# Out projections and a pooling layer's input projection by seven products of quarters

## The chip, the cores and the metric

The kernel runs on one core of a Trainium2 chip. A core has a matrix engine (TensorE, PE in the profile; loading its stationary side is PEld), three engines that work on tiles in the on-chip memory SBUF (VectorE or DVE, ScalarE or ACT, GpSimd or POOL), and a queue engine (SyncE or SP) that here only starts transfers. Products go to a second memory, PSUM, which the matrix engine writes and VectorE and ScalarE read. The metric is the device time of one execution in microseconds.

## What is computed

Two layers over 1,024 tokens of 2,048 channels. Everything below concerns the two output projections and the second layer; the attention in front stays as it is but for what it leaves in DRAM.

```python
def _attention_layer(...):                      # layer 0
    ...
    y = jnp.concatenate([outA, outB], axis=-1) * jax.nn.silu(z)
    x = x + gate * _rmsnorm(y @ w_out, post_g)

def _pool_layer(...):                           # layer 1
    h = _rmsnorm(x, pre_g) * (1 + scale) + shift
    proj = h @ w_in                             # 2048 -> 4096: u and the gates
    y = _multiscale_pool(proj[..., :POOL_WIDTH], pool_w, pool_scale) * jax.nn.silu(proj[..., POOL_WIDTH:])
    x = x + gate * _rmsnorm(y @ w_out, post_g)

def _multiscale_pool(u, pool_w, pool_scale):    # windows 2, 4, 8, 16 for four groups of 512 channels
    ...                                         # centred mean over the window, less the token
    mixed = jnp.einsum('blgc,gcd->blgd', pooled, pool_w).reshape(B, L, POOL_WIDTH)
    return mixed * pool_scale
```

All numbers are float32.

## The kernel before

A product of two float32 matrices is made of three products of 12-bit parts: each side is split into a high part (a cast to fp32r on ScalarE, in `split`, L146) and a low part (the number less its high part, on VectorE or GpSimd, L149), and `PASSES` takes high by high, high by low and low by high.

Weights come from DRAM in `w_tiles`: up to 1,024 columns at a time into a raw tile `wr` (two buffers), split into `wh` and `wl` (eight buffers each). The layer before attention goes through `gemm` (L186) over blocks of 256 outputs.

Attention runs over 32 units (four groups of heads, eight blocks of 128 queries). Each unit turns weights (L850), multiplies them with the values (L904), multiplies the result by the gate over the softmax's sums (`gate_over_sums` on GpSimd, `gated` on VectorE), splits it into `yo` and stores both parts to DRAM (`yd`). The softmax's sums go by DRAM too: `ls` is stored to `lsd` and read back as `rs` on all partitions.

`out_proj` (products on L962) is called for each half of the tokens, 512 at a time: four column groups of 512, each over 16 chunks of 128 rows and four blocks of tokens, with the tokens stationary and 512 weight columns moving. Its end multiplies by the gate (L969), squares for the norm, and adds the residual (L1026 or L1149). After layer 0 the rows are normed (L1033), turned (L1062) and split again into `hT`; six blocks of layer 1's first gates (L1043) stand between, so that the second half's turning has products beside it. Layer 1 (`project1`, `pooled`) goes through `gemm` for both halves of the tokens at once, so each weight is read and split once. `pooled` adds by doubling (L1106) on VectorE and GpSimd in turn; the pool maps (`mx`) are products of `gemm` as well, and their result goes to DRAM as `y1d`.

A scheduler places the instructions on each engine; `keep_in_program_order` holds some of them in the order of the code. Loads stand in SyncE's queue (`load`), stores mostly in ScalarE's (`store`).

Of the kernel before, what the change touches and what calls it, by code (L numbers as in the profile page):

```python
# [17 lines left out]
P = 128  # L18
D = 2048
# [4 lines left out]
HL = L // NH  # L24
HD = 128
# [5 lines left out]
# A product of two float32 numbers, each cut exactly into two 12-bit parts.  # L31
# [4 lines left out]
LEAD = 28  # L36
# [9 lines left out]
BRIDGE = 6  # L46
PINS = (0,)
# Chunks of rows whose products ACT and Pool take, for shifts and scales.
# [3 lines left out]
def _constants():  # L52
# [7 lines left out]
    # Blocks of keys before, at and after the queries' own; the context's are all open.  # L60
# [18 lines left out]
def tile_backbone(ctx, tc, ins, out):  # L79
# [4 lines left out]
    # Sums of the modulation over the rows, still to be added up over the partitions.  # L84
# [19 lines left out]
    # Which of four lots of partitions a partition belongs to.  # L104
# [24 lines left out]
    # Scratch in DRAM.  # L129
# [8 lines left out]
    yd = [[dram([P, 4, 2, HL], f"yd{g}_{n}") for n in range(NH)] for g in range(4)]  # L138
    gpd = [[dram([1, 512], f"gpd{i}_{j}") for j in range(4)] for i in range(2)]
    x1d = [dram([P, D], f"x1d{t}") for t in range(8)]  # L140
    sd = [dram([P, HL], f"sd{m}") for m in range(BRIDGE)]
    y1d = [[dram([P, 4, 2, HL], f"y1d{g}_{n}") for n in range(NH)] for g in range(4)]

# [7 lines left out]
    wp = pool(ctx, "w")  # L151
# [39 lines left out]
    def newton(r, v, t):  # L191
        """r = 1 / sqrt(v), with a Newton step; t is room for it."""
# [7 lines left out]
    def rstd_rows(r, ss, tp, n, tag):  # L200
        """r = 1 / sqrt(ss / D + eps), elementwise."""
# [4 lines left out]
    def lots_of(d, a):  # L206
        """512 columns of d, as lots of 32 partitions with 128 columns of four of d's rows each."""
# [10 lines left out]
    # ---------------------------------------------------------------- attention weights  # L218
# [3 lines left out]
    # The pools of the units with an even number and, later, those with an odd one.  # L222
# [14 lines left out]
    def scores(u, kt, s_tile, c_tile, pinned=lambda i: i, pin=lambda i: i, band=None):  # L237
        """Attention weights of four heads' blocks of queries, with queries on the partitions."""
# [53 lines left out]
    # ---------------------------------------------------------------- layer 0: norms and projections  # L292
    with ExitStack() as st:
# [13 lines left out]
        # Small vectors, one column per 128 channels.  # L307
# [15 lines left out]
        # Scales and shifts of the attention layer's tokens, 512 channels at a time: products with the rows of the  # L323
        # weights, which the partitions add up first.
# [16 lines left out]
        def mod_add(accs, k, w, c, tp, shared):  # L341
            """Adds a chunk's products, on DVE or, the shared ones, on ACT and Pool."""
# [14 lines left out]
        def mod_columns(accs, n=4):  # L357
            """The sums over the partitions, a column per 128 channels."""
# [25 lines left out]
        # Tokens scaled by their root mean squares, then with channels on the partitions.  # L384
# [32 lines left out]
        def project(c0, nm, beside=None):  # L417
            """Products of blocks c0.. of w_in's columns with the tokens, by (block, half), with others between them."""
# [15 lines left out]
        def three(c0):  # L434
            """Three blocks, by halves, and the weights' tiles, two chunks of rows at a time."""
# [7 lines left out]
        # The first blocks of queries are made without the shifts, which come later and are added to the products.  # L443
# [79 lines left out]
        def rotated(src, n, g=None):  # L523
            """The rotary turn of a head's columns, times g."""
# [259 lines left out]
    def act_tile(k, n):  # L784
        """A chunk of 128 channels of one half of the tokens, in two parts."""
        return acts[n, k // 8].tile([P, 2, HL], F32R, tag="a", name="a")
# [392 lines left out]
```

## Time and profile before

| | |
|---|---|
| median of the runs (3) | 3113.52 us (3113.2 to 3115.45) |
| span of the profiled execution | 3115.6 us |
| PE busy | 2989.6 us (96%), 14,102 products |
| DVE busy | 1649.9 us (53%) |
| ACT busy | 1075.0 us (35%) |
| POOL busy | 424.1 us (14%), 327 instructions |
| DMA | 530.34 MB, mean 170 GB/s |

The page gives the busy time of each engine over one profiled execution. A matrix engine busy for 96% is a busy sequence of products, each of which overlaps the next; how long one takes in a sequence is read from the starts of its neighbours. Layer 0's projections and the modulation end near 1,140 us, attention near 1,605, the first out projection near 2,032, layer 1's projections near 2,756.

### The profile page before, as it was taken

How to read it: one execution, taken by the hardware profiler on the slowest of the kernel's cores; microseconds unless marked ns; L12 is line 12 of the kernel's file. 1: busy time of each engine (PE TensorE's matmuls, PEld its weight loads, DVE VectorE, ACT ScalarE, POOL GpSimd, SP SyncE). 2: the span in 40 equal slices, each digit the busy share in tenths (PEclk: the TensorE clock that was granted, in tenths of full speed). 3: DMA queues.
4: the chain of work that ended last, by engine and by line, in shares of the span. 5: the costliest groups of instructions: out<-in, count | busy, mean ns of one | idle time of the engine just before them, and what ended most of it. 6: DMA issues, size and time to landing. Idle time of an engine off the chain costs nothing.

```text
span 3115.6 us, 38559 instructions
## 1 busy us (share of the span) xinstructions
PE 2989.6 (96%) x14102; PEld 2481.0 (80%) x14102; DVE 1649.9 (53%) x2725; ACT 1075.0 (35%) x2073; POOL 424.1 (14%) x327
## 2 busy tenths in 40 slices
PE   5899999899999999999899999999999999999998
PEld 5677777787888788888778888888888888888887
DVE  7968877555235748888753363623332323322434
ACT  6542312221111147776642352522222221222332
POOL 4643413000001100001220040300000001000000
PEclk8989999999999999999999999999999999999999
DMA  8738776888467854445555544423222121355734
GB/s 289 242 126 252 215 247 219 254 289 260 171 235 253 267 177 124 136 125 159 153 170 164 214 138 157 156 65 111 85 91 75 48 101 49 129 176 172 250 104 163
DMA packets 373011, 530.34 MB, mean 170 GB/s; under 512 B 28644, under 2 KB 215894, under 8 KB 371670
## 3 DMA queue, kind: packets, MB, share of 16 engines
q1 hardware_dynamic: 287990, 445.81, 44.7%
q10 hardware_dynamic: 84832, 82.07, 7.7%
q8 instruction: 111, 1.82, 0.2%
q14 instruction: 78, 0.64, 0.1%
HBM read 428.88 MB, written 98.91 MB: 169 GB/s over the span
## 4 chain that ended last, share of the span: by engine, by line
PE 70%; DMA 13%; DVE 9%; issue 3%; ACT 2%; POOL 2%; SPq 0%; ACTq 0%; DVEq 0%; POOLq 0%
PE g L186 32%; PE g L962 21%; DMA mraw<-in_od_mod_w_dram 5%; DVE mac L355 5%; PE o L904 4%; DMA mraw<-in_ev_mod_w_dram 3%; PE mx L186 3%; PE s L254 3%; PE t L850 3%; PE g L1043 2%; DVE wl L149 1%; DMA lsd<-ls 1%; DMA wr<-in_od_w_out_dram 1%; DMA rs<-lsd 1%; PE c L260 1%
## 5 line engine op out<-in xcount | busy, mean ns | idle before, releaser
L149 DVE TENSOR_TENSOR wl<-wr,wh 128x512 fp32r<-128x512 f32 (+1 forms) x576 | 414.9, 726 | 852.6 <-ACT wh L146 835.4
L186 PE MATMUL g<-h,wh 128*128 128x512 f32 x2368 | 756.8, 400 | 8.1 <-ACT fe L477 5.8
L146 ACT CAST wh<-wr 128x512 fp32r<-128x512 f32 (+1 forms) x576 | 349.6, 615 | 1100.2 <-PE g L186 563.5
L962 PE MATMUL g<-wh,a 128*128 128x512 f32 x1920 | 594.4, 390 | 0.1
L186 PE MATMUL g<-a,wh 128*128 128x512 f32 x1856 | 571.0, 389 | 0.0
L186 PEld LDWEIGHTS g<-h,wh 128*128 128x128 f32 x2368 | 453.9, 194 | 100.7 <-POOL h L148 5.9
L186 PE MATMUL g<-h,wl 128*128 128x512 f32 x1184 | 473.9, 401 | 14.2 <-DVE wl L149 14.1
L355 DVE SCALAR_TENSOR_TENSOR mac<-mraw,csil,mac 128x512 f32<-128x512 f32 x423 | 364.5, 862 | 120.2 <-DMA mraw<-in_od_mod_w_dram 64.8
L962 PEld LDWEIGHTS g<-wh,a 128*128 128x128 f32 x1920 | 360.1, 188 | 75.5 <-ACT wh L146 0.8
L186 PEld LDWEIGHTS g<-a,wh 128*128 128x128 f32 x1856 | 348.3, 188 | 72.4
L962 PE MATMUL g<-wl,a 128*128 128x512 f32 x960 | 373.7, 389 | 0.0
L186 PE MATMUL g<-a,wl 128*128 128x512 f32 x928 | 360.7, 389 | 0.0
L186 PEld LDWEIGHTS g<-h,wl 128*128 128x128 f32 x1184 | 227.9, 193 | 67.0 <-DVE wl L149 19.9
L962 PEld LDWEIGHTS g<-wl,a 128*128 128x128 f32 x960 | 180.2, 188 | 37.2
L186 PEld LDWEIGHTS g<-a,wl 128*128 128x128 f32 x928 | 174.2, 188 | 36.3
L149 DVE TENSOR_TENSOR tl<-t,th 128x512 fp32r<-128x512 f32 x236 | 160.0, 684 | 39.5 <-ACT th L146 38.0
L146 ACT CAST th<-t 128x512 fp32r<-128x512 f32 x236 | 135.9, 584 | 110.6 <-PE t L850 109.3
L904 PE MATMUL o<-th,vt 128*128 128x512 f32 x472 | 156.3, 412 | 2.5 <-ACT th L146 2.5
L850 PE MATMUL t<-ident,p 128*128 128x128 f32 x944 | 139.0, 276 | 10.5 <-DVE tl L149 10.1
L850 PEld LDWEIGHTS t<-ident,p 128*128 128x128 f32 x944 | 114.8, 142 | 38.2 <-DVE tl L149 15.5
L537 POOL TENSOR_TENSOR ra<-ra,rt 128x512 f32<-128x512 f32 x40 | 64.7, 1619 | 553.1 <-DMA mraw<-in_ev_mod_w_dram 287.8
L1106 POOL TENSOR_TENSOR s<-s 128x541 f32<-128x541 f32 (+1 forms) x32 | 38.1, 1190 | 587.4 <-DVE s L1106 561.7
(221 smaller groups left out, 3357.2 us busy)
## 6 DMA issues: line engine op xcount, KB each, us to landing
mraw<-in_ev_mod_w_dram SPq DMA_DIRECT2D x192, 256.0 KB, 4.0
mraw<-in_od_mod_w_dram SPq DMA_DIRECT2D x192, 256.0 KB, 4.6
wr<-in_od_w_in_dram SPq DMA_DIRECT2D x76, 512.0 KB, 3.6
wr<-in_ev_w_in_dram SPq DMA_DIRECT2D x68, 512.0 KB, 4.6
mraw<-in_ev_mod_w_dram SPq DMA_DIRECT2D x64, 512.0 KB, 5.2
wr<-in_ev_w_out_dram SPq DMA_DIRECT2D x64, 512.0 KB, 3.8
wr<-in_od_w_out_dram SPq DMA_DIRECT2D x64, 512.0 KB, 4.8
qd<-hl ACTq DMA_DIRECT2D x64, 256.0 KB, 2.9
```

What stands on the lines that cost most here:

```text
L146: nc.scalar.copy(dst_h, src)
L149: (lo or nc.vector).tensor_tensor(dst_l, src, f32(dst_h), op=ALU.subtract)
L186: pin(nc.tensor.matmul(o, lhsT=w[a][:, kk, m * P : (m + 1) * P], rhs=rhs(n, k, b), start=(k == 0 and i == 0), stop=(k == kc - 1 and i == 2),))
L254: pin(nc.tensor.matmul(s[:, sl], lhsT=qt[:, h, a], rhs=kt[:, b, sl], start=i == 0, stop=i == 2))
L260: pinned(nc.tensor.matmul(cs[:, hh], lhsT=qt[:, h + hh, a], rhs=kt[:, b, L:], start=i == 0, stop=i == 2))
L355: nc.vector.scalar_tensor_tensor(accs[0], w, c, accs[0], op0=ALU.mult, op1=ALU.add)
L537: nc.gpsimd.tensor_tensor(a, a, t, op=ALU.add)
L850: pin(nc.tensor.transpose(t[:, h * P : (h + 1) * P], ps[h][:, i * P : (i + 1) * P], ident))
L904: pin(nc.tensor.matmul(outs[u], lhsT=vt[:, a, kb], rhs=b, start=(i == 0 and jj == 0), stop=(last and jj == 2)))
L962: nc.tensor.matmul(o, lhsT=y[k][:, a, t * P : (t + 1) * P], rhs=wt[b][:, k - k0, :], start=(k == 0 and i == 0), stop=(k == KC - 1 and i == 2),
L1043: mm = nc.tensor.matmul(o, lhsT=w[a][:, k - k0, m * P : (m + 1) * P], rhs=hT[k][0][:, b], start=(k == 0 and i == 0), stop=(k == KC - 1 and ...
L1106: eng.tensor_tensor(nx[:, lo + d :], cur[:, lo + d :], cur[:, lo : W - d], op=ALU.add)
```

## The change

Each of the out projections and layer 1's input projection is made of seven products of quarters in place of eight (the Strassen scheme in Winograd's form), over halves of the tokens. A block of 512 tokens, 512 outputs and all 2,048 rows is cut in two along each side. The left side then has eight slots, of which seven are used: four quarters of the tokens and four sums of them. The right side has seven: four quarters of the weights and sums of them. `seven` makes the products, 256 columns each, and adds them up out of seven PSUM banks.

The left sides go through DRAM (`ad`): attention, the turning of the normed tokens and the pool maps store their quarters and sums there (`left_sums`, on GpSimd), and `left_part` loads and splits them beside the last seven of the step before. `weights_of` makes the sums of the weights on GpSimd. Since one half of the tokens is done at a time, layer 1's weights are loaded and made twice. Gates and pooled tokens of layer 1 go through DRAM too (`gd`, `pod`), the pool maps stand between the projections' products (`map_steps`), and the rows' ends (`Beside`) beside the next out projection or the gates.

```diff
+    def left_sums(v):
+        for o, a, b, op in ((4, 6, 7, ALU.add), (2, 4, 0, ALU.subtract), (3, 0, 6, ALU.subtract), (5, 1, 2, ALU.subtract)):
+            nc.gpsimd.tensor_tensor(v[o], v[a], v[b], op=op)
...
         def gated(u, o, zt):
-            y = ap.tile([P, 4 * P], F32, tag="y", name="y", bufs=1)
-            nc.vector.tensor_tensor(y, o, zt.rearrange("p h q -> p (h q)"), op=ALU.mult)
-            yo = ap.tile([P, 2, 4 * P], F32R, tag="yo", name="yo", bufs=1)
-            split(yo[:, 0], yo[:, 1], y, "act", nc.gpsimd if u >= YP else None)
-            for t in range(2):
-                load(yd[g][n // 4][:, :, t, (n % 4) * P : (n % 4 + 1) * P], f32(yo[:, t]).rearrange("p (h q) -> p h q", q=P))
+            tp, ti = n % 2, n // 2 % 2
...
+            nc.vector.tensor_tensor(
+                sa[:, :, 6 * ti : 6 * ti + 2, :], o.rearrange("p (k i q) -> p k i q", k=2, i=2),
+                zt.rearrange("p (k i) q -> p k i q", k=2), op=ALU.mult,
+            )
+            if ti:
+                left_sums([sa[:, :, i, :] for i in range(8)])
+                for k in range(2):
+                    load(ad[0][n // 4][g // 2][:, 2 * (g % 2) + k, :, tp * P : (tp + 1) * P], sa[:, k])
...
+    def left_part(d, q):
+        left_tiles(q)
+        for s0 in range(0, 8, 2):
+            raw = staged()
+            slots = [s for s in (s0, s0 + 1) if s != 6]
+            for s in slots:
+                load(raw[:, 2 * (s - s0) : 2 * (s - s0) + 2], d[q // 2][:, 2 * (q % 2) : 2 * (q % 2) + 2, s, :])
+            for s in slots:
+                a = left[s][q]
+                v = raw[:, 2 * (s - s0) : 2 * (s - s0) + 2].rearrange("p k t -> p (k t)")
+                split(a[:, 0], a[:, 1], v, lo=nc.gpsimd if s % 2 else None)
+    def weights_of(w, kp, c0):
+        raw = wq.tile([P, 2, 2, QT], F32, tag="wr", name="wr", bufs=3)
...
+        t = wq.tile([P, 3, QT], F32, tag="wt", name="wt", bufs=2)
+        for o, a, b, op in (
+            (t[:, 1], raw[:, 1, 1], raw[:, 1, 0], ALU.subtract),
+            (t[:, 0], t[:, 1], raw[:, 0, 0], ALU.add),
+            (raw[:, 1, 0], raw[:, 1, 0], raw[:, 0, 0], ALU.subtract),
+            (t[:, 2], raw[:, 0, 1], t[:, 0], ALU.subtract),
+        ):
+            nc.gpsimd.tensor_tensor(o, a, b, op=op)
+        for i, v in ((0, raw[:, 0]), (2, t[:, 0:2]), (1, raw[:, 1]), (3, t[:, 2:3])):
+            made[i] = split_weights(v)
+    def seven(w, c0, tokens_still, q, done):
+        banks = [psg.tile([P, 2, QT], F32, tag="g", name="g") for _ in SEVEN]
+        for kp in range(8):
+            parts = weights_of(w, kp, c0)
+            for i, (slot, tile_, place) in enumerate(SEVEN):
+                a, o = left[slot][kp // 2], banks[i]
+                for v in range(2):
+                    for n_, (x, y) in enumerate(PASSES):
...
+                        tc.keep_in_program_order(nc.tensor.matmul(
+                            o[:, v], lhsT=lhsT, rhs=rhs, start=(kp == n_ == v == 0), stop=(kp == 7 and n_ == 2), skip_group_check=True,
+                        ))
+                if kp == 7:
...
+                        add(q(0, 0), o, q(1, 0), op=ALU.add)
...
+    def out_proj(ev, w, gps, ss, og):
...
+                for tp in range(2):
+                    square(ev, c[:, tp], ss[:, 2 * ti + tp, cp : cp + 1])
+                nc.gpsimd.tensor_tensor(c, c, gp.to_broadcast([P, 2, HL]), op=ALU.mult)
...
+    def attention_turn(ev, n, og):
+        for kp in range(8):
+            for tp in range(2):
+                sa = staged().rearrange("p a (b t) -> p (a b) t", b=2)
...
+                left_sums([sa[:, i] for i in range(8)])
+                to = ad[1][n][kp // 4][:, kp % 4, :, tp * P : (tp + 1) * P]
+                store(to[:, 0:6], sa[:, 0:6])
+                store(to[:, 7], sa[:, 7])
+                yield
...
+        for cp, kp in out_proj(ev, w_outs[0], gpd[0], ss, og):
+            if cp == 3 and kp % 2:
+                left_part(ad[1][0] if n else ad[0][1], kp // 2)
+            beside()
+        beside.set(attention_rows(ev, n, ss, og), attention_turn(ev, n, og))
```

The weights have two tags: double tiles `wh`, `wl` of 512 columns with four buffers and single ones of 256 with one (`WBUFS = 1, 4`); the staging tiles (`xr`) have two, `left` one per slot and quarter.

The order of the instructions at three places. TensorE at the end of attention, before (o are the attention's products; g the out projection's, with 512 weight columns moving):

```order
L904 MATMUL o<-th,vt 128x512 x2
L904 MATMUL o<-tl,vt 128x512
L962 MATMUL g<-wh,a 128x512
L962 MATMUL g<-wl,a 128x512
L962 MATMUL g<-wh,a 128x512 x2
```

And after (a_14553 to a_14555 are the first three slots of the left side):

```order
L913 MATMUL o<-th,vt 128x512 x2
L913 MATMUL o<-tl,vt 128x512
L1021 MATMUL g<-wh,a_14553 128x256
L1021 MATMUL g<-wl,a_14553 128x256
L1021 MATMUL g<-wh,a_14553 128x256 x2
L1021 MATMUL g<-wl,a_14553 128x256
L1021 MATMUL g<-wh,a_14553 128x256
L1021 MATMUL g<-wh,a_14554 128x256
```

The same place in the sequence now has six products of 256 columns per slot, two blocks of three passes.

GpSimd from the end of attention to the second half of the tokens, before (zt and yo are attention's; og the normed rows; a the turned tokens):

```order
L866 TENSOR_TENSOR zt<-zt,rs 128x512
L149 TENSOR_TENSOR yo<-y,yo 128x512
L1033 TENSOR_SCALAR og<-og,s_15887 128x512 x4
L1033 TENSOR_SCALAR og<-og,s_15929 128x512 x4
L1033 TENSOR_SCALAR og<-og,s_15971 128x512 x4
L1033 TENSOR_SCALAR og<-og,s_16013 128x512 x4
L148 TENSOR_SCALAR a<-nw 128x512 x16
```

And after, in the first out projection's last seven of the first half (wt and wr are the weights' sums, a_ the left side's low parts, og<-og,gp the gate):

```order
L1092 TENSOR_TENSOR og<-og,gp 128x1024
L998 TENSOR_TENSOR wr<-wr 128x256
L152 TENSOR_TENSOR a_16499<-xr,a_16499 128x512
L998 TENSOR_TENSOR wt<-wr,wt 128x256
L998 TENSOR_TENSOR wt<-wr 128x256
L152 TENSOR_TENSOR a_16501<-xr,a_16501 128x512
L998 TENSOR_TENSOR wt<-wt,wr 128x256
L998 TENSOR_TENSOR wr<-wr 128x256
L998 TENSOR_TENSOR wt<-wr 128x256
L152 TENSOR_TENSOR a_16502<-xr,a_16502 128x512
```

Where GpSimd had nothing between attention and the first norms, it now has the sums of every step's weights, with the left side's low parts among them.

SyncE's queue in the last units of attention, before (ls, rs: the softmax's sums; yd: the gated result; zt: a later unit's gate):

```order
L289 DMA lsd_153<-ls 128x4
L876 DMA yd_1_163<-yo 512x1x128
L918 DMA rs<-lsd_153 128x512
L876 DMA yd_1_163<-yo 512x1x128
L865 DMA zt<-zd_1_123 128x512
L289 DMA lsd_154<-ls 128x4
```

And after, from the same unit on, to the start of the out projection (ad: the left sides; xr: their staging tiles; gp: the gate; wr: the weights):

```order
L293 DMA lsd_153<-ls 128x4
L927 DMA rs<-lsd_153 128x512
L865 DMA zt<-zd_1_123 128x512
L293 DMA lsd_154<-ls 128x4
L927 DMA rs<-lsd_154 128x512
L293 DMA lsd_155<-ls 128x4
L927 DMA rs<-lsd_155 128x512
L1080 DMA gp<-gpd_0_156 128x512
L885 DMA ad_1_1_175<-sa 128x8x128 x4
L974 DMA xr<-ad_0_0_172 128x2x256 x5
L990 DMA wr<-in_ev_w_out_dram 128x2x256
```

The store that stood between a unit's lsd and rs now stands behind rs, and the first loads of the left side stand behind attention's last stores.

## Rows read from the trace of the kernel before

**Rows 1.** Busy time by stretch: start:end, length, each engine, granted clock, DMA share.
```profile
1400.00:1600.00 200.00, 183.72 (x1130) 159.36 (x1128) 149.60 (x372) 136.42 (x329) 43.48 (x31) 0.98 0.52 148
1607.00:3107.00 1500.00, 1498.64 (x6658) 1237.41 (x6656) 541.90 (x946) 428.79 (x799) 99.74 (x99) 1.00 0.39 131
3107.00:3116.00 9.00, 0.00 (x0) 0.00 (x0) 3.98 (x12) 0.89 (x3) 0.00 (x0) 0.72 0.33 127
```

**Rows 2.** The chain that ended last, pieces: start us, length us, what.
```profile
1542.15 4.66 DMA yd<-yo
1548.77 4.11 DMA lsd<-ls
...
1607.28 191.04 PE g L962 x842
...
2144.58 11.19 PE mx L186 x48
```

**Rows 3.** Timeline of TensorE near 905 us: start us, length, what.
```profile
902.05 0.63 PE L186 MATMUL g<-h,wh 128*128 128x512 f32 x2
...
907.51 0.40 PE L186 MATMUL g<-hc,wh 128*128 128x256 f32 x2
...
908.93 0.63 PE L186 MATMUL g<-h,wh 128*128 128x512 f32 x2
```

**Rows 4.** Instructions of single lines: duration ns least/median/most, first and last start.
```profile
L149 DVE TENSOR_TENSOR wl<-wr,wh x576: 545/691/1783, 44.8 to 3052.3; 128x512 fp32r<-128x512 f32 x181, 128x384 fp32r<-128x384 f32 x11
L149 DVE TENSOR_TENSOR tl<-t,th x236: 659/685/693, 1146.2 to 1605.4; 128x512 fp32r<-128x512 f32 x118
L149 POOL TENSOR_TENSOR hl<-ra,hl x40: 1268/1676/1842, 245.2 to 1079.1; 128x512 fp32r<-128x512 f32 x40
L149 POOL TENSOR_TENSOR hl<-zt,hl x4: 737/966/1191, 938.8 to 1080.7; 128x256 fp32r<-128x256 f32 x4
L537 POOL TENSOR_TENSOR ra<-ra,rt x40: 1260/1726/2321, 242.9 to 1076.6; 128x512 f32<-128x512 f32 x40
L148 POOL TENSOR_SCALAR h<-nw x32: 611/1048/1160, 143.0 to 219.6; 128x512 fp32r<-128x512 f32 x32
L1026 DVE SCALAR_TENSOR_TENSOR og<-og,sm,a x32: 747/1094/1185, 1786.8 to 1994.9; 128x512 f32<-128x512 f32 x32
L1106 POOL TENSOR_TENSOR s<-s x32: 1087/1088/1839, 2228.3 to 2665.1; 128x541 f32<-128x541 f32 x24, 128x529 f32<-128x529 f32 x8
```

**Rows 5.** Timelines of POOL and DVE over 174 to 184 us.
```profile
175.85 2.07 POOL L148 TENSOR_SCALAR h<-nw 128x512 fp32r<-128x512 f32 x2
177.89 6.46 POOL L350 TENSOR_TENSOR max<-max,mpr 128x512 f32<-128x512 f32 x4
...
176.35 2.11 DVE L149 TENSOR_TENSOR h<-nw,h 128x512 fp32r<-128x512 f32 x2
178.38 1.75 DVE L355 SCALAR_TENSOR_TENSOR mac<-mraw,csil,mac 128x512 f32<-128x512 f32 x1
180.05 3.17 DVE L149 TENSOR_TENSOR wl<-wr,wh 128x384 fp32r<-128x384 f32 x2
```

**Rows 6.** Groups by line and shape: busy us, mean ns; idle before, releasers.
```profile
L146 ACT CAST wh<-wr 128x512 fp32r<-128x512 f32 x544 | 334.1, 621 | 1086.6 <-PE g L186 549.8 <-PE g L962 303.9 <-DMA wr<-in_od_w_out_dram 48.9
L1106 DVE TENSOR_TENSOR s<-u 128x543 f32<-128x543 f32 x32 | 23.1, 721 | 40.1 <-ACT u L1096 39.4
L1106 POOL TENSOR_TENSOR s<-s 128x529 f32<-128x529 f32 x8 | 11.6, 1451 | 7.6 <-DVE s L1106 7.6
```

**Rows 7.** Timelines of POOL and DVE at a block of rows, near 1992 us.
```profile
1992.10 5.01 POOL L1033 TENSOR_SCALAR og<-og,s 128x512 f32<-128x512 f32 x4 [5.45 <-DVE sm L198]
...
1992.07 3.97 DVE L1026 SCALAR_TENSOR_TENSOR og<-og,sm,a 128x512 f32<-128x512 f32 x4
```

**Rows 8.** Transfers by line: issuing queue, count, KB each, median us to landing.
```profile
zt<-zd SPq DMA_DIRECT2D x32, 256.0 KB, 3.7
x1d<-og ACTq DMA_DIRECT2D x32, 256.0 KB, 2.5
```

More of the change, by code (lines that the diff above doesn't have):

```diff
@@ L149, in split @@
         (lo or nc.vector).tensor_tensor(dst_l, src, f32(dst_h), op=ALU.subtract)
-    wp = pool(ctx, "w")
+    s_wp = ExitStack()
+    wp = pool(s_wp, "w")
     def w_tiles(w, cols, kc=KC, hi="act", room=None):
@@ L1014, in other_half @@
[L1014 to L1029 removed]
+    parts_in = [pool(ctx, f"parts{q}") for q in range(4)]
@@ L1073, in tile_backbone, with map_steps @@
+    ready, loaded = [], []
+    def map_steps(kp):
+        if kp == 7 and ready:
+            loaded.append(ready.pop(0))
+            run(loaded[0])
+        elif 2 < kp < 7 and loaded:
+            run(loaded[0])
+            if kp == 6:
+                loaded.pop()
+    for s in range(4):
+        for kp in gates(s, ev):
+            beside()
+    beside.end()
+    s_ev.close()
     with ExitStack() as st:
-        ev = pool(st, "ev2")
-        edge = ev.tile([P, 64], F32, name="edge")
+        mp = pool(st, "maps")
+        edge = mp.tile([P, 64], F32, name="edge", bufs=1)
@@ L1142, in tile_backbone @@
[L1142 to L1153 removed]
+        tails = mp.tile([P, 8, 2, 16], F32, name="tails", bufs=1)
@@ new lines, in tile_backbone @@
+        maps = iter(())
+        with ExitStack() as st_u:
+            up = pool(st_u, "u", side="right")
+            for g in range(4):
+                for kp in channels(g, 0, up):
+                    if g == 3 and kp % 2:
+                        left_part(ad[1][1], kp // 2)
+            for g in range(4):
+                for kp in channels(g, 1, up):
+                    map_steps(kp)
+                ready.append(mapped(mp, g, 0))
+        zp = pool(st, "gates", side="right")
+        for s in range(4):
+            z = zp.tile([P, 2, 2, 2, QT], F32, tag="z", name="z", bufs=2)
+            for kp in silu_gates(s, 1, lambda ti, j: z[:, ti, j], lambda ti, j: None):
+                map_steps(kp)
+                if s == 3 and kp % 2:
+                    left_part(ad[2][0], kp // 2)
+            ready.append(mapped(mp, s, 1, z, psg if s > 1 else pst))
@@ new lines, in tile_backbone, with layer_end @@
+        for m in loaded + ready:
+            run(m, 99)
+    ev = pool(ctx, "ev3", side="right")
+    def layer_end(n, ss, og, rows=None):
+        for t in range(4):
+            for cg, r, xr in finished(ev, t, ss, x1d[4 * n + t], rows and rows[2 * t : 2 * t + 2]):
+                v = og[t // 2][cg][:, t % 2]
+                if rows and cg == 1:
+                    nc.scalar.activation(v, v, AF.Copy, scale=r)
+                    nc.gpsimd.tensor_tensor(v, v, xr, op=ALU.add)
+                else:
+                    nc.vector.scalar_tensor_tensor(v, v, r, xr, op0=ALU.mult, op1=ALU.add)
+                (load if cg % 2 else store)(out[0][(4 * n + t) * P : (4 * n + t + 1) * P, cg * HL : (cg + 1) * HL], v)
+            yield
@@ L1157 @@
+    beside.end()
 _INS = [
```

432 lines of the change are left out of this document (233 added, 199 removed).

## The prediction

> **What bounds the kernel now.** I read the table of stretches first: from 1607 us, where the first out projection begins, to 3107 us the matrix engine is busy 1498.6 of 1500 us at a granted clock of 1.00 (2.4 GHz), while VectorE works 542 us and GpSimd 100 us [rows 1]. The chain of waits agrees: in that half it runs nearly all along products, like the 842 of L962 in a row from 1607.28 [rows 2]. So this half is bound by the number of products, and an edit that takes products away is worth their time, as long as nothing else becomes the bound. What could is read from the rows on VectorE and GpSimd.
>
> **What the change takes away.** Before, an out projection or layer 1's input projection costs 192 products of 512 columns per 512 tokens and 512 outputs; there are 32 such blocks, 6144 products. The timeline of the matrix engine has 24 of them from 902.05 to 907.51: 0.2275 us each, 1397 us in all. After, `seven` makes 8 steps of 42 products of 256 columns. Products of 256 columns, each with its own weight load, stand in the same timeline: 12 from 907.51 to 908.93, 0.1183 us each [rows 3]. That is slightly over half, and the ratio of work is 7/8. A step takes 42 x 0.1183 = 4.97 us, a block ("a seven") 39.7 us, all 32 take 1272 us. The pool maps stay: eight pieces of 48 products at 11.19 us [rows 2], 90 us. The 128 transposes (14 us) stay too. **On the matrix engine alone 125 us go.**
>
> **What it adds, and to whom.** Nearly all new work is on GpSimd, 1,700 instructions for 330. Per step `weights_of` makes four sums of 256 columns there, and ScalarE and VectorE split seven quarter tiles where a step had eight before in bigger pieces. Prices alone, without a neighbour, are the least of each row [rows 4]: GpSimd's two-input op takes 1.27 us at 512 columns and 0.74 at 256 (so 0.21 and 2.07 ns a column: an estimate of 2.33 at 1024 and 0.47 at 128); VectorE's subtraction 0.69 at 512 and 0.55 at 384, so 0.41 at 256. ScalarE's casts are 0.62 each [rows 6], 2.3 us a step, and it touches nothing that the others wait for; I leave it at nothing, covered by the 4.97 us of products.
>
> **The two engines do not work side by side.** This decides the case. Where VectorE subtracts SBUF from SBUF while GpSimd works, each of VectorE's ops is stretched: the subtraction goes from 0.69 to 1.78 us at most, GpSimd's ra from 1.26 to 2.32. Where VectorE's other input lies in PSUM (tl<-t,th) nothing is stretched (0.693 at most) [rows 4]. Rows that alternate give the price of a pair: GpSimd's scaling (0.62 alone) with a subtraction of 0.69, two pairs from 176.35 to 178.38, 1.02 each; GpSimd's sum of 1.27 with an op of 0.75, from 178.38 to 180.05, 1.67 [rows 5]. So a pair that meets takes its sum less about 0.3 us. The new subtractions (raw and high part, both in SBUF) are of the stretched kind; the additions out of PSUM in `seven` are not.
>
> One step then costs this shared path 4 x 0.74 + 3 x 0.69 + 0.41 = 5.44, less four times 0.3: **4.24 us of the 4.97** that its products take. A seven needs 33.9 us of 39.7, and with the out projection's two gate products of 1024 columns on GpSimd (2 x 2.33 less 0.3) 38.3. Weights are buffered for one step and a third (four double tiles), so what goes over is a stall of the matrix engine soon after.
>
> **Where it goes over.** Left parts: a quarter is four subtractions of 512 on GpSimd and three on VectorE, 5.08 + 2.07 - 0.9 = 6.25 us, four quarters 25. There are six. Four stand in out projection sevens: 38.3 + 25 - 39.7 = 23.6 each, 94. One stands beside the last `channels` of the first half, whose own sums take 14 (GpSimd's 1.09 and VectorE's 0.72 and 0.75, doubled with the width [rows 4, 6]): 33. One beside the last gates, with a map in it (11.2 us more of products, 9 of the path): 17. **144 us.** The order on GpSimd shows them between the sums of the weights, not behind them.
>
> Rows of the attention layer: a block of four scalings and four multiply-adds holds both engines for some 4.3 us (VectorE's four take 3.97, GpSimd's 5.01 with a subtraction behind [rows 7]); four blocks in one seven are 17: 15.6 over in the out projection, 11.2 in the gates, **27 us**. They also wait for the stores of x1d (2.5 us to landing [rows 8]) with the weights' sums behind them in GpSimd's queue; covered if the scheduler placed them late enough. Turned tokens: four sums of 128 per step make GpSimd's own time 2.96 + 1.88 + 0.58 = 5.42 per step, 43.4 a seven, and half of its meetings with VectorE add 4: 8 over in two sevens, 3 in two others, **22 us**; the transposes hide there. The other `channels` and the last layer's rows: **23 us**. Sum over: 216 us, more than the 125 that go.
>
> Ends. The attention's last 16 units wait for transfers: the chain has yd<-yo in place of rs<-lsd at some units [rows 2]. The new order on SyncE has lsd and rs in a row, the store behind them, and ScalarE's cast of yo is gone. There are 16 us of idle time in 1400 to 1600 [rows 1] to win; I take 6, and the bounds are 0 and 16. The start of the out projection now waits behind the attention's last sums: four of 0.74 on GpSimd, then the lower parts a1 and a3 (1.27 each), then loads that land in 3.7 us [rows 8] and were queued on SyncE behind the last stores. Before, 2 us were lost there; I take 8 more, bounds 3 and 15. At the end four blocks of rows finish together where before one did (9 us from 3107 on [rows 1]): two gate products, 12 multiply-adds of 0.75 [rows 4], four short norms, the last store: 20 us.
>
> **Sum.** 1607 - 6 + 8 = 1609; products 1272 + 90 = 1362; over 216; end 20: a span of 3207, against 3115.6 of the profiled execution. The median of the runs, 3113.5, is 2 us under that span: **3205 us**, 2.9% slower.
>
> **Bounds.** GpSimd has one cheaper row: L1106 adds 541 columns in 1.087, 1.62 ns a column [rows 4]. Its inputs are one tile shifted by two columns; at a shift of eight the same line takes more (the 529-column form is among the slower ones, mean 1.45 [rows 6]). The new sums read inputs that lie apart, like the rows at 2.07, and I take those. At 1.62 a step costs the path 3.78, a left part 21, and what goes over is 124 with 10 for transposes: 3123 us. Upward, the sevens of the out projection leave 1.4 us of 39.7 free; if evictions (seven of 0.69 on VectorE in the last step) hold up the weights by 2 us in each seven, 64 more: 3270.
>
> **Rivals.** *Products decide after all (faster).* Its place are the handovers: if GpSimd's and VectorE's work were pulled ahead over the sevens with spare time, or the pairs overlapped, only starts and ends would stall: 1609 + 1376 + five handovers of 5 + 20 - 2 = 3028. For it: averaged over the half, 1,400 us, GpSimd's own ops sum to some 1,110 and VectorE's to 1,035, so neither is full by itself. Against it: the pairs of [rows 5], by which the path's sum is near 1,500, and buffers of a step and a third. It decides from a pair price of the sum less 0.5: then some 109 us go over, and with the worse ends that just eats the 125.
> *GpSimd cheaper:* 3123, as above.
> *Queues in order make it worse.* Each of the 32 turn steps stores from ScalarE's queue, waiting for GpSimd's sums, with the casts of the weights queued behind. If each costs 3 us: 3300. For it: ScalarE's casts now wait 550 us for products [rows 6], so its waits cost nothing; then they would.
> *No overlap at all.* If pairs took their full sum, a step would cost 5.44, over the products in every seven; the path's ops sum to 1,950 us and the time is 3577. The rows of pairs, 1.02 for 1.31 and 1.67 for 2.02, speak against it. The Trainium skill has this as a rule (SBUF — State Buffer, "Who interferes with whom"): a VectorE instruction with two SBUF inputs and a GpSimd one that reads SBUF share a read port by an exclusive lock, and the loser blocks for the whole instruction. By that rule's letter this change is a loss whatever the products give; the trace agrees on who blocks whom, but each op's first 0.1 to 0.2 us lies outside the lock.
>
> **How the numbers follow.** Within 0.2% (6 us) a measurement of this kernel can't tell a difference. Forecast 0.60, its own range 3150 to 3290; GpSimd cheaper 0.12 (faster 0.04, same 0.02, slower 0.06); products decide 0.17, faster; queues 0.08 and no overlap 0.03, slower. Faster 0.21, same 0.02, slower 0.77. The range 3085 to 3310 leaves out the products' case and the last.
>
> **What would show it.** After, VectorE's subtractions of the weights should average well over 0.69 us (0.9 to 1.1), `weights_of`'s sums over 0.74 (1.0 to 1.1); stretches with a left part should take 60 us and more per seven with the matrix engine idle for a third, waiting for wl, the lower parts and wt; plain sevens should take 40. GpSimd busy over 75% from 1610 us on. Products of 256 columns every 0.118 us. I am wrong if sevens with left parts take 40 to 45 us, or if the sums of 256 take 0.55 us.

## The result, and the profile after

The changed kernel takes 3375.01 us (median of 4, 3374.28 to 3378.87) against 3114.48 (3113.2 to 3118.12) beside it on the same chip: a ratio of 1.0837, 95% interval 1.0822 to 1.0853. The sign of the forecast was right; the size was not, 3205 with a range that ended at 3310. The kernel before took 3112 to 3121 us beside the runs below, so a few us between two of them say nothing.

The table of stretches of the changed kernel, with the columns of [rows 1]. The first row runs from the first product of a `seven` to the last; the others are single sevens (336 products each): two plain ones, one with a left part, the one behind it (rows of the attention layer beside it), the same behind the second half of the tokens, one with a map, the last gates with three maps.

```profile
1623.00:3347.00 1724.00, 1500.09 (x11265) 1441.75 (x11265) 1410.75 (x1654) 819.53 (x1586) 1456.98 (x1399) 0.94 0.51 160
...
1692.00:1733.80 41.80, 41.16 (x339) 40.56 (x339) 37.45 (x41) 20.88 (x42) 39.64 (x37) 1.00 0.35 108
1733.80:1774.90 41.10, 40.77 (x338) 40.37 (x337) 36.76 (x40) 20.82 (x42) 38.29 (x34) 1.00 0.36 109
1774.90:1826.10 51.20, 44.62 (x338) 42.47 (x337) 48.12 (x46) 28.59 (x58) 49.14 (x40) 0.97 0.53 160
1826.10:1900.70 74.60, 48.39 (x342) 45.68 (x341) 67.69 (x116) 38.17 (x87) 67.61 (x61) 0.83 0.64 202
...
2061.60:2138.70 77.10, 48.38 (x343) 46.11 (x341) 69.04 (x117) 41.26 (x93) 67.55 (x60) 0.82 0.63 205
...
2692.10:2759.00 66.90, 56.37 (x385) 51.86 (x385) 55.71 (x61) 22.62 (x40) 52.16 (x46) 0.95 0.48 154
...
2871.00:2978.90 107.90, 84.71 (x481) 75.22 (x482) 71.62 (x86) 48.44 (x85) 71.98 (x71) 0.85 0.61 195
```

Where the matrix engine was busy 1498.6 of 1500 us before, it is now short of work: GpSimd is busy 1457 of 1724 us and VectorE 1411, and in the sevens with a left part or rows (51 to 77 us) both are busy for some nine tenths of the time. Of these rows the plain sevens alone have a clock of 1.00. Now look at one step of a plain seven, on both engines (start us, length us, engine, line, operation, shapes; the four sums of the weights on GpSimd, the low parts on VectorE):

```profile
1708.38 1.19 POOL L998 TENSOR_TENSOR wt<-wr 128x256 f32<-128x256 f32 x1
1709.53 1.18 POOL L998 TENSOR_TENSOR wt<-wr,wt 128x256 f32<-128x256 f32 x1
1710.67 1.19 POOL L998 TENSOR_TENSOR wt<-wt,wr 128x256 f32<-128x256 f32 x1
1711.82 0.92 POOL L998 TENSOR_TENSOR wr<-wr 128x256 f32<-128x256 f32 x1
1712.69 1.19 POOL L998 TENSOR_TENSOR wt<-wr,wt 128x256 f32<-128x256 f32 x1
```

```profile
1709.10 2.15 DVE L152 TENSOR_TENSOR wl<-wr,wh 128x512 fp32r<-128x512 f32 x2
1711.18 0.95 DVE L152 TENSOR_TENSOR wl<-wt,wh 128x256 fp32r<-128x256 f32 x1
1712.54 0.74 DVE L152 TENSOR_TENSOR wl<-wt,wh 128x512 fp32r<-128x512 f32 x1 [0.40 <-ACT wh L149]
1713.42 1.00 DVE L152 TENSOR_TENSOR wl<-wr,wh 128x512 fp32r<-128x512 f32 x1
```

Sums of 0.72 us take 1.19, subtractions of 0.69 take up to 1.22, and they take turns, as in [rows 5]. The chain of waits (start us, length, what) in the same seven has GpSimd's sums every 4.3 us:

```profile
1708.38 3.48 POOL wt L998 x3
1712.69 2.34 POOL wt L998 x2
1717.01 2.34 POOL wt L998 x2
1721.33 2.40 POOL wt L998 x2
```

A step is thus 4.32 us of the shared path; the forecast said 4.24.

To see how far this goes I put all of VectorE's and GpSimd's instructions together, VectorE's with an input from PSUM left out (those are not stretched: 0.67 to 0.68 us each in the row below), and worked out three numbers from their starts and ends: the sum of what they would take alone (each at the least of its kind in this trace), the time in which at least one of the two is busy ("occupied"), and how often the path changes from one engine to the other in order of ends.

```profile
L1036 DVE TENSOR_TENSOR og<-g,og x20: 673/676/681, 1693.7 to 3346.6; 128x512 f32<-128x512 f32 x20
```

| stretch | length, us | sum alone | occupied | changes |
|---|---|---|---|---|
| plain seven from 1733.8 | 41.2 | 46.9 | 39.7 | 59 |
| with a left part, from 1774.9 | 51.2 | 59.4 | 50.4 | 72 |
| the one behind it, from 1826.1 | 74.6 | 91.3 | 74.2 | 102 |
| first turns, from 1900.7 | 55.5 | 61.6 | 53.1 | 58 |
| all 32, 1623 to 3347 | 1724 | 1898 | 1622 | 2056 |

So the two engines together are occupied 1622 of 1724 us, and that is the sum alone less 276 us: 0.134 for each of the 2056 changes.

### The profile page after: what moved, and what is told of

The parts are those of the page before. It is cut to its first block, busy times and chain, and to the rows that moved or that the text cites. A ratio compares the mean times of both kernels' runs of the same rounds, so it can differ in the third digit from the quotient of the medians.

```text
span 3372.5 us, 53623 instructions
## 1 busy us (share of the span) xinstructions
PE 2996.1 (89%) x18710; PEld 2681.9 (80%) x18710; DVE 2530.0 (75%) x3449; ACT 1456.1 (43%) x2845; POOL 1830.1 (54%) x1689
## 3 DMA queue, kind: packets, MB, share of 16 engines
q14 instruction: 124, 1.02, 0.1%
## 4 chain that ended last, share of the span: by engine, by line
PE 17%; POOL 14%; issue 9%; DVE 8%; DMA 4%; ACT 1%; SPq 0%; DVEq 0%; ACTq 0%; POOLq 0%
PE g L1021 14%; POOL wt L998 7%; DVE wl L152 3%; POOL xr L794 2%; PE mx L1237 2%; DMA wr<-in_od_w_in_dram 1%; POOL a L152 1%; POOL wr L998 1%; DMA po<-pod 1%; POOL og L1092 1%; DMA xr<-ad 1%; POOL og L1127 1%; DVE a L152 1%; ACT wh L149 1%; DVE og L1309 1%
## 5 line engine op out<-in xcount | busy, mean ns | idle before, releaser
L152 DVE TENSOR_TENSOR wl<-wr,wh 128x512 fp32r<-128x512 f32 (+1 forms) x712 | 711.8, 1017 | 242.7 <-ACT wh L149 212.9
L1021 PE MATMUL g<-wh,a 128*128 128x256 f32 x3584 | 684.3, 291 | 42.6 <-ACT wh L149 17.0
L1021 PE MATMUL g<-a,wh 128*128 128x256 f32 x3584 | 674.7, 290 | 27.4 <-ACT wh L149 14.8
L1021 PE MATMUL g<-a,wl 128*128 128x256 f32 x1792 | 525.1, 293 | 62.6 <-DVE wl L152 61.9
L152 DVE TENSOR_TENSOR wl<-wt,wh 128x512 fp32r<-128x512 f32 (+1 forms) x512 | 469.4, 928 | 143.6 <-ACT wh L149 125.7
L1021 PE MATMUL g<-wl,a 128*128 128x256 f32 x1792 | 525.9, 294 | 35.6 <-DVE wl L152 32.4
L149 ACT CAST wh<-wt 128x512 fp32r<-128x512 f32 (+1 forms) x512 | 260.2, 512 | 400.5 <-POOL wt L998 185.3
L998 POOL TENSOR_TENSOR wt<-wr 128x256 f32<-128x256 f32 x256 | 259.3, 1013 | 185.6 <-DVE wl L152 113.0
L998 POOL TENSOR_TENSOR wt<-wr,wt 128x256 f32<-128x256 f32 x256 | 274.4, 1072 | 0.0
L998 POOL TENSOR_TENSOR wr<-wr 128x256 f32<-128x256 f32 x256 | 265.1, 1036 | 0.0
```

The costliest lines, as they stand in the source:

```text
L149: nc.scalar.copy(dst_h, src)
L152: (lo or nc.vector).tensor_tensor(dst_l, src, f32(dst_h), op=ALU.subtract)
L998: nc.gpsimd.tensor_tensor(o, a, b, op=op)
L1021: tc.keep_in_program_order(nc.tensor.matmul(o[:, v], lhsT=lhsT, rhs=rhs, start=(kp == n_ == v == 0), stop=(kp == 7 and n_ == 2), skip_grou ...
```

## The experiments

**Who does the sums.** All sums of the weights on VectorE:

```diff
-            nc.gpsimd.tensor_tensor(o, a, b, op=op)
+            nc.vector.tensor_tensor(o, a, b, op=op)
```

> The weights' four sums per step go from GpSimd to VectorE, the same work otherwise. Shared path (GpSimd and VectorE exclude each other, their sum decides): GpSimd's 0.74 becomes an estimated 0.41 on VectorE, but the 0.3 us that a pair saved is gone too, so a step costs 4.1 us for 4.2 and little is won: sevens with nothing beside them fall from 41.2 to about 40 us, those with left parts, rows or turns by 1 to 3 us each, 3375 to about 3340 (3310 to 3360). Rival, GpSimd's own slowness (its sums wait in its own queue behind low parts, gates and rows, and the weights with them): taking 1,024 of its 1,700 instructions off its queue frees it, the sevens with left parts, rows and turns fall to 40 to 50 us, the time to about 3200. VectorE's subtractions of the weights should fall from a mean of 0.93 to 1.02 us to near 0.69 wherever GpSimd is idle, in both.

3360.7 us (one run): 14 less, where 35 were expected by the shared path and 175 by its rival. GpSimd's slowness or its queue by itself is not what sets the time. The sums cost 0.40 to 0.43 us there (second row; least, median, most in ns):

```profile
L998 DVE TENSOR_TENSOR wt<-wr x256: 404/425/2616, 1164.4 to 3319.9; 128x256 f32<-128x256 f32 x128
L998 DVE TENSOR_TENSOR wt<-wt,wr x256: 406/419/1512, 1165.6 to 3320.4; 128x256 f32<-128x256 f32 x128
```

Plain out projection sevens are at 42.0 to 42.7 us, with VectorE busy 35 to 38 of it, evictions out of PSUM included. The first of them in the table of stretches:

```profile
1701.70:1743.70 42.00, 40.79 (x339) 40.41 (x338) 37.57 (x71) 20.99 (x42) 5.04 (x2) 1.00 0.35 107
```

So the path is not full there; the later steps of this seven follow each other every 5.04 us, the time of their 42 products. That is the part of the expectation that failed: counted as below, the two engines are occupied some 220 us less than in the changed kernel, and 14 us came out. Where the gain went, by sevens: behind a left part VectorE alone is busy nearly all the time (67.7 of 70.3 us in the one that took 74.6), and the six sevens with maps take 416 us for 410.

**No sums at all.** The sum tiles go, and the splits read raw quarters:

```diff
-        t = wq.tile([P, 3, QT], F32, tag="wt", name="wt", bufs=2)
-        for o, a, b, op in (
...
-            nc.gpsimd.tensor_tensor(o, a, b, op=op)
-        for i, v in ((0, raw[:, 0]), (2, t[:, 0:2]), (1, raw[:, 1]), (3, t[:, 2:3])):
+        for i, v in ((0, raw[:, 0]), (2, raw[:, 0]), (1, raw[:, 1]), (3, raw[:, 1, 1:2])):
```

> Left out: the sums of the weights (the splits read the raw quarters in their place, so ScalarE and VectorE do as many and as big splits as before, and the products are the same). Shared path: a step's path is VectorE's 2.5 us, all sevens without a left part go to about the products' 39.7 to 42 (51 to 53 with a map), those with one stay at about 50 with what spills into the next; 3375 to about 3090 (3060 to 3140). If it is loads, stores, or the order of queues that holds the sevens up, they keep most of their 50 to 77 us and the time stays over 3250.

3221.8 us (one run): 153 less, but not the 285 expected. Plain sevens stand at 40.3 us, 0.120 for each of 336 products. What is left above 40.3 (and 11.2 a map) is 188 us: 21 in the first seven, 81 in four left parts with the seven behind each, 28 in the sevens with turns, 52 in those with maps, the rest small. Either theory of the expectation was too simple: the sums of the weights are on the path, and without them other waits hold 130 us more than I gave them.

**What the exclusion hangs on.** The weights' low parts from one input:

```diff
-        split(h, l, v)
+        nc.scalar.copy(h, v)
+        nc.vector.tensor_scalar(l, v, 1.0, 1.0, op0=ALU.mult, op1=ALU.mult)
```

> The weights' low parts are written by VectorE from one input in SBUF (a scaled copy of the raw tile, in place of raw less high), so the low parts are not low parts; everything else is there, the sums on GpSimd too. Tells what the exclusion hangs on. If it needs VectorE's second SBUF input: GpSimd's sums stand at 0.74 again where they meet only these copies, a step's path is GpSimd's 2.96 us, and the time falls to about 3120 (3080 to 3180). If an op of one SBUF input excludes GpSimd as well: GpSimd's sums keep a mean near 1.0 us, and the time falls only by what the copies are shorter than the subtractions.

3272.9 us (one run). Rows of both lines (ns least, median, most):

```profile
L984 DVE TENSOR_SCALAR wl<-wr x544: 407/714/2694, 1163.4 to 3238.7; 128x512 fp32r<-128x512 f32 x182
...
L999 POOL TENSOR_TENSOR wt<-wr x256: 719/742/1832, 1164.3 to 3234.0; 128x256 f32<-128x256 f32 x128
...
L999 POOL TENSOR_TENSOR wr<-wr x256: 717/916/1767, 1165.8 to 3236.0; 128x256 f32<-128x256 f32 x128
```

VectorE's op of one input is short, 0.41 us for 512 columns, but half of them take over 0.71, up to 2.69. GpSimd's sums are stretched less than before: two of the four have a median of 0.74, the other two of 0.92, where the changed kernel had 1.07 to 1.18. So the outcome lies between the two that were expected. The exclusion does not need a second input, since an op with one SBUF input waits here too, and the time fell because the copies are shorter: by themselves 242 us in all, of which 102 came out at the end. By the Trainium skill (SBUF — State Buffer, "Who interferes with whom") an op in a two-port mode is in the lock as well. This run agrees with that if the copy is such an op: it takes 0.41 us for 512 columns where the subtraction takes 0.69, but no row shows the mode itself.

**The maps' products.** Two of twelve kept in each bank:

```diff
-                for k in range(4):
-                    for n_, (x_, y) in enumerate(PASSES):
+                for k in (0, 3):
+                    for n_, (x_, y) in ((0, PASSES[0]),):
...
```

> Left out: 10 of the 12 products of each bank of the pool maps (40 of 48 products a piece, 75 us of the matrix engine over all eight pieces); what VectorE, ScalarE, GpSimd and the transfers do for the maps stays. The forecast priced a seven with a map at its products, 51 us, and it took 54 to 67. If the work beside the products decides there: the three sevens of 60 to 67 us stay within 3 us, those of 54 and 58 fall by 3 to 8, and the time by 20 to 40, to about 3345. If the products decide: every seven with a map falls by 9, the time by 75 to about 3300.

3346.2 us (one run), 29 less for 75 us of products. The three sevens of 60 to 67 us fell by 4.5 to 7.3, not by under 3, those of 54 and 58 by 3 and not at all, the last with three maps by 25; the seven behind that took 8.6 back. Occupied time stayed at 1616. So neither side is right alone: with a map, a seven is held up by both the path and the products.

**The transposes' wait.** The turns four steps later:

```diff
-            else:
+            elif self.tick > 11:
                 run(self.turns)
```

> The turning of the normed rows begins four steps later, after both out projections, and nothing else changes. In the changed kernel TensorE stands 34.8 us in front of four transposes whose rows GpSimd has not scaled yet, with the products queued behind them. If that wait costs its time: 3375 falls by 25 to 35 us, to about 3345. If the shared path of GpSimd and VectorE sets the time (it is idle for at most 3 us in each of these sevens), it is the same wait that would else stand at the weights: the time falls by 0 to 5 us.

3379.6 us (median of 4, 3371.98 to 3380.37), ratio 1.0835 (1.0818 to 1.0853): no change. Waits of the matrix engine (engine, line, waited for: us in total, times, longest) in the second half of the changed kernel, and then of this one:

```profile
PE g L1021 <- DVE wl L152: 94.2, 87, 3.8
PE t L1139 <- POOL og L1127: 34.8, 4, 16.1
```

```profile
PE g L1021 <- DVE wl L152: 102.7, 96, 3.9
...
PE t L1139 <- ACT xr L1142: 13.6, 1, 13.6
...
PE t L1139 <- POOL og L1127: 5.0, 1, 5.0
```

The wait for the scaled rows fell by 30 us (the transposes' other wait, for ScalarE, rose from 5.2 to 13.6) and nothing was won. The sevens show where it went: the two with rows fell from 74.6 and 77.1 to 59.3 and 59.5, and the six that follow them rose from 301.2 to 328.2: 6 us less for the eight together. The waits moved with the work.

**Low parts of the left sides on VectorE.**

```diff
-                split(a[:, 0], a[:, 1], v, lo=nc.gpsimd if s % 2 else None)
+                split(a[:, 0], a[:, 1], v)
```

> The left parts' four low parts a quarter that were on GpSimd go to VectorE. Shared path: a left part's 16 subtractions cost 1.27 us less about 0.2 where they meet, 17 us; on VectorE 0.69 each, 11: 6 us less in each of the six left parts, 3375 to about 3340 (3330 to 3350), and it shows in the seven with the left part and the one behind it together. Rival, two engines are better than one (the lows on GpSimd run beside VectorE's): no gain or a loss, 3370 to 3400.

3350.2 us (one run), 25 less for 35 expected. The first seven and the four pairs of a left part with the seven behind it lost 5.2, 6.6, 6.7, 5.7 and 5.6 us, the 6 of the expectation; the sixth left part, at the last gates, lost nothing: its seven waits for something else.

**The clock.** Transposes into an idle bank behind each slot's products, in six sevens:

```diff
+                    for e in range(extra):
+                        tc.keep_in_program_order(nc.tensor.transpose(spare[:, e * P : (e + 1) * P], ident, ident))
...
```

> In six sevens that wait most (the first, the one behind each left part, and the last channels of the first half) two or four transposes of 0.11 us into an idle bank stand behind each slot's six products: 12 or 24 us more work for TensorE in each, 110 in all, where it stood idle for 19 to 37. In these sevens the granted clock was 0.78 to 0.94 and up to 72 of 336 products took 0.21 us in place of 0.12. If the low clock costs time: it rises to near 1.00, and these sevens become 5 to 10 us shorter each in spite of the work, 3375 to about 3335. If the shared path sets the time and the clock only follows: these sevens stay within 2 us, the time at 3370 to 3385.

3400.8 us (median of 4), ratio 1.0912 (1.0894 to 1.093). The two sevens of 74.6 and 77.1, with 24 us more for the matrix engine each, in the table of stretches:

```profile
1826.00:1900.00 74.00, 65.71 (x529) 64.10 (x528) 63.98 (x101) 39.44 (x90) 64.70 (x58) 0.95 0.65 210
2061.00:2138.00 77.00, 68.79 (x564) 67.13 (x564) 65.94 (x109) 38.95 (x91) 69.42 (x61) 0.98 0.63 203
```

Clock 0.95 and 0.98 for 0.83 and 0.82, and their lengths 74.8 and 73.8: 0.2 longer and 3.3 shorter, where the expectation had 5 to 10 shorter for a costly clock. In the other four (the first seven went from 68.8 to 78.2) the extra work cost 4 to 9 us. The extra work and the higher clock came together, so this run alone does not part the two; that the low clock is no more than a follower here is told by the run with a third of the products, below, whose second half is shorter at a clock of 0.66.

**A third buffer for the second gates.**

```diff
-            z = zp.tile([P, 2, 2, 2, QT], F32, tag="z", name="z", bufs=2)
+            z = zp.tile([P, 2, 2, 2, QT], F32, tag="z", name="z", bufs=3)
...
```

> The tiles that hold layer 1's second gates until the pool maps use them get a third buffer (a small table moves to another pool to make room). In the changed kernel TensorE waits 4.6, 5.3 and 4.6 us in the last two gate sevens for evictions into these tiles, in sevens where the weights' sums made no difference (54, 58 and 108 us, and 54, 58 and 103 without sums). If these waits set the time there: 3375 falls by 8 to 15 us. If the shared path does: under 3 us.

3375.2 us (median of 4), ratio 1.0828 (1.0812 to 1.0844): no change, though the seven of 58.0 fell to 53.4.

**Less on GpSimd.** The row scaling, the gate and the left parts' low parts moved:

```diff
-                nc.gpsimd.tensor_scalar(row[cg], row[cg], s2[:, 5:6], 1.0, op0=ALU.mult, op1=ALU.mult)
+                nc.scalar.activation(row[cg], row[cg], AF.Copy, scale=s2[:, 5:6])
...
-                nc.gpsimd.tensor_tensor(c, c, gp.to_broadcast([P, 2, HL]), op=ALU.mult)
+                nc.vector.tensor_tensor(c, c, gp.to_broadcast([P, 2, HL]), op=ALU.mult)
...
```

> The rows' scaling goes from GpSimd to ScalarE, the left parts' low parts and the out projections' gate from GpSimd to VectorE. Shared path, priced as the runs so far show it (the ops' own times, less about 0.14 us for each change from one engine to the other): the lows gave 25 us by themselves; the scaling is 22 us of GpSimd off the path less 9 of changes lost, the gate 70 less 37 on VectorE less 8, of which half lies in sevens that the path holds up: 3350 to about 3320 (3305 to 3335). If a work taken off GpSimd comes free of charge (its own queue was what waited): 3280 or less. Whether any such shift of work can reach the kernel before is answered by the run without the weights' sums: 3222.

3323.1 us (median of 4), ratio 1.0656 (1.0638 to 1.0674). The price of 0.14 for a change forecast 3320; 25 of the 52 us were known from the run with the low parts on VectorE, so it is the other 27 that test it.

**A third of the products.**

```diff
-                    for n_, (x, y) in enumerate(PASSES):
+                    for n_, (x, y) in enumerate(PASSES[:1]):
...
```

> Left out: two of the three passes of each product in the sevens, so TensorE has a third of the 1,272 us of them; both parts of both sides are made as before. Shared path: GpSimd's and VectorE's occupied time of about 1,620 us stays, only what both stood idle (some 100 us) and the ends can shrink: 3375 to about 3290 (3250 to 3330). If the products and the stalls in their order (transposes, evictions, half clock) made the time: the second half would fall to less than 1,000 us, the time to 2600 or less.

3320.6 us (one run). In the table of stretches, over the length from the first product to the last (1664 us; the row begins 6 us behind the first):

```profile
1633.00:3297.00 1664.00, 917.18 (x4088) 777.64 (x4088) 1445.17 (x1657) 797.12 (x1591) 1452.09 (x1396) 0.66 0.52 164
```

7,168 of 10,752 products are gone and 54 us with them. VectorE and GpSimd are as busy as before, 1445 and 1452 us, and occupied for 1595 of 1664 us. So neither the products nor the low clock (0.66 here) bounds the second half; what is left is the two engines' work, which fills all but 69 us of it.

**The best that cheap sums could give.** The edits of the runs without sums and with less on GpSimd, together:

> Left out: the weights' sums, as in the run without them; the rows' scaling is on ScalarE, the left parts' low parts and the gate on VectorE. How far the change could get if its weights' sums cost nothing and the rest shared the path least. Without sums the plain sevens stand at the products' 40.3 us and about 170 us of waits are left, of which the left parts with what follows them hold some 80; the three moves should take 25 to 45 us of those: 3222 to about 3185 (3170 to 3200), still above the kernel before. If the shared path was the whole of the rest: 3120 or less.

3187.0 us (median of 4), ratio 1.0226 (1.0209 to 1.0243). Even with its sums for nothing and less on GpSimd the change loses to the kernel before; no version here beat it.

The sums in one table (us; per change in ns), for six kernels with sums on GpSimd:

| kernel | first to last product | sum alone | occupied | changes | saved per change |
|---|---|---|---|---|---|
| changed kernel | 1724 | 1898 | 1622 | 2056 | 134 |
| two map products | 1692 | 1899 | 1616 | 2097 | 135 |
| turns later | 1721 | 1903 | 1617 | 2065 | 138 |
| lows on VectorE | 1694 | 1846 | 1571 | 1908 | 144 |
| less on GpSimd | 1671 | 1791 | 1534 | 1787 | 144 |
| a third of the products | 1664 | 1895 | 1595 | 2123 | 142 |

The run with low parts from one input has about 1,650 us alone, 1,420 occupied of 1,616 and 0.12 a change. In the runs with the sums on VectorE, without them, and without them with less on GpSimd, the two engines are occupied for only some 1,406 of 1,702, 1,088 of 1,568 and 997 of 1,539 us: that leaves 300 to 540 us in which the products or other waits set the time.

## Why the prediction was wrong in size

**Shared path: right for the changed kernel, but not one for one.** VectorE and GpSimd exclude each other, and their work fills the second half: the run with a third of the products shows that it is not the products. A shorter path gives less than its length, since other waits stand close behind it: with the low parts on VectorE and with less on GpSimd the path lost 51 and 88 us and the second half 30 and 53. VectorE's subtractions average 0.93 to 1.02 us and GpSimd's sums 0.98 to 1.07, as the last part of the forecast asked (0.9 to 1.1 and 1.0 to 1.1). Two of the page's groups (shapes, count, busy us, mean ns, idle before):

```profile
L152 DVE TENSOR_TENSOR wl<-wr,wh 128x512 fp32r<-128x512 f32 (+1 forms) x712 | 711.8, 1017 | 242.7 <-ACT wh L149 212.9
...
L998 POOL TENSOR_TENSOR wt<-wr 128x256 f32<-128x256 f32 x256 | 259.3, 1013 | 185.6 <-DVE wl L152 113.0
```

The prices that were estimated from two rows held too: 256 columns on VectorE 0.41 (0.40 measured), 1024 on GpSimd 2.33 (2.34).

**The step that failed: "a pair that meets takes its sum less about 0.3 us", given to every instruction of GpSimd.** [rows 5] show pairs that alternate strictly, two changes of engine each. The forecast's path was 1950 us of work less 450, so 1,500. Measured: 1898 less 276, so 1622. The work was 52 too high; the saving was 174 too high, because 1399 instructions of GpSimd make 2056 changes and not 2798 (two or three sums in a row have none between them), and a change saves 0.134 and not 0.15. In plain sevens the savings nearly held (a step of 4.32); in turns, with 65 GpSimd instructions and 58 changes, they did not. There the forecast had 43.4 us of GpSimd's own and 4 for meetings, and GpSimd (the last engine of the row) is busy 51.7:

```profile
1900.70:1956.30 55.60, 48.32 (x371) 47.48 (x369) 33.43 (x41) 30.74 (x66) 51.72 (x67) 0.92 0.49 150
```

**And a second step: "what goes over" taken as the longer of path and products.** The forecast's term of 216 us over the products measured 345, if a seven's products are taken at 40.3 us and a map's at 11.2. By place:

| place | forecast over | measured over |
|---|---|---|
| left parts, rows, other channels, all else | 177 | 223 |
| four sevens with turns | 22 | 43 |
| six sevens with maps | 17 | 79 |

The largest miss, 62 us, lies in the sevens with maps. The forecast put five of them at their products, 51 us (what it had for channels, some of them beside a map, is in the first row). Each of the six took longer than its products and longer than its path: 60, 63, 67, 54, 58 and 108 us, with the two engines occupied for some 53, 57, 63, 47, 51 and 90.

All of the 165 us by which the span missed (3372.5 for 3207), by differences, which is a reckoning and not four causes shown: path 122; time in which the path is idle 24 (102 for the 78 that the forecast's 1578 us left); start 14; end 5 (25.2 for 20).

**Start.** The forecast won 6 us in attention's last 16 units. Units 15 to 31 did win 12 (by the starts of `gate_over_sums`: 31.2 us behind the kernel before at unit 15, 18.6 at unit 31). But the units ahead of them lost 31, and the forecast had looked at none of these. There, products wait for the low part of the turned weights, 42 times and 20 us in all, where the kernel before had 4 such waits. The row of the list of waits over 1140 to 1450 us (us in total, times, longest):

```profile
PE o L913 <- DVE tl L152: 20.0, 42, 0.8
```

The timeline of VectorE around 1297 us has `tl` behind the 1.23 us of a row maximum. That the new order on VectorE makes this loss was not tried by a run. The first product of the out projection, put 8 us later, came 0.6 us behind the last gate, for 3.2 before.

**Places.** Left parts were priced together with the seven behind them about right: the first pair takes 125.8 us, the forecast's parts 63.3 and 55.3 make 118.6. But I had the delay inside the seven with the left part ("60 us and more") and most of it is behind it, 51.2 and 74.6: 10 of the left part's 28 casts on ScalarE start only there, the last 29 us into it. What holds them back was not tried. Sevens with maps took 54 to 67 us for 51, and the last 108 for 90 (its products, three maps and 17 over). There the path is idle 4 to 18 us a seven. Neither the products alone, the weights' sums nor the gates' buffer is what holds them: the run without sums still has 54, 58 and 103 us in the last three. That remainder stays open; the chain of waits (start us, length, what) has loads of the pooled tokens there, which no run took away:

```profile
2932.98 8.53 DMA po<-pod
2943.12 12.58 PE mx L1237 x47
2955.71 7.64 DMA po<-pod
```

The second of these loads starts where the products of the map before it end (2943.12 and 12.58 make 2955.70); both buffers of the pooled tokens (`po`) belong to that map. A third pair of them would test it.

**Transposes and clock.** The forecast hid the transposes and said nothing of the clock. Both show in the trace (34.8 us of waits; some 620 products at 0.21 us for 0.12), and by the runs with later turns and with a third of the products neither costs time by itself: the path is busy meanwhile.

**Products.** 0.120 us each and not 0.1183: 18 us over 10,752, which count only where the matrix engine isn't waiting anyway.

**Rivals.** *Products decide* falls with the third of the products. *GpSimd cheaper* falls by its least: 0.714 us for 256 columns, where that rival's price makes 0.63. *Queues in order* gave the nearest number, 3300. Its reason has little room: in the first turns the path is occupied 53.1 of 55.5 us, and the four sevens with turns are 43 us over their products where it needs 96 more. No run took the stores off ScalarE's queue. *No overlap* at 3577 was 202 us too much, the forecast 170 too little: the truth lay between the two prices, and the range should have had a case for meetings that happen less often than once an instruction.

## What to carry to other kernels

Before giving GpSimd a job beside VectorE, add up both engines' SBUF work as one queue and take off some 0.14 us for each change between them (the figure of six kernels of this program), counted from the order, not one pair for each instruction; then compare with what bounds the stage. Where the two come close, expect a stage to take longer than either. Savings on an engine that stops being the bound are gone: 7/8 of the products was worth less than the sums that buy it. A wait or a low clock of the matrix engine is a price only if the engine that it waits for is idle then; look at that first.

## What was not expected of the hardware

A scaled copy from one input in SBUF (0.41 us for 512 columns by itself) meets GpSimd's exclusion as the subtractions from two do, up to 2.69 us. Keeping the matrix engine busy brought the granted clock from 0.83 to 0.95 and from 0.82 to 0.98, and the two sevens, where it waited for data, took 0.2 us more and 3.3 less.
